# An experts' stage on TensorE: its order written down, and its weights read in longer rows

## The chip, the cores and the metric

The kernel runs on one core of a Trainium2 chip. The metric is device time of one execution in microseconds. The kernel before takes 2113.49 us, the median of three runs (2113.06 to 2113.59).

Engines are called by their short names in the profile: PE is TensorE (PEld its loading of the stationary operand), DVE is VectorE, ACT is ScalarE, POOL is GpSimd, SP is the engine that issues nearly all DMAs.

## The reference, cut to what matters

Two transformer-like blocks follow each other on 512 tokens of width 1024, all in float32. The first block (attention of two kinds, then a mixture of experts) holds the change. Its experts' part, per token block:

```python
    grp_probs = jax.nn.softmax(jnp.dot(x2, w_rg).astype(jnp.float32) + b_rg.astype(jnp.float32), axis=-1)
    grp = jnp.argmax(grp_probs, axis=-1)
...
    top_val, top_idx = lax.top_k(in_grp, TOP_K_IN_GROUP)
    gate = jax.nn.softmax(top_val, axis=-1) * p_grp[:, None]
...
    def run_block(args):
        tok, g, e = args
        xb = x2[tok]
        hb = jax.nn.silu(xb @ w_gate[e]) * (xb @ w_up[e])
        return (hb @ w_down[e]) * g[:, None].astype(x2.dtype)
...
    return jnp.zeros_like(x2).at[slot_tok].add(y_blocks.reshape(n_slots, -1))
```

`x2` is the normalised residual (`rmsnorm(h, g_ffn)`). Each token takes the best 2 of the 8 experts of its best group, of 4 groups; there are 32 experts, `run_block` is done on the tokens of one of them, `w_gate` and `w_up` are 1024 x 512 for each, `w_down` is 512 x 1024. The result is added to the residual `h`.

## The kernel before, in words

**Tiling.** The residual `h` is kept on chip, 4 chunks of 128 tokens by 1024 columns. Each expert has 64 places for tokens; a branch (L1246) with a general loop stands by for an expert that gets more, and is not taken with these inputs. The stage (`moe`, L1174) works on two experts at once, `p` from 0 to 15 (L1393): expert `2p` in columns 0 to 63 of the PE array, expert `2p+1` in columns 64 to 127, each product written with its place (`tile_position`). One product of a column half is two PE instructions in the trace, since the data is float32.

**One pass.**
- On even `p`: `onehots` (L1359) makes on DVE the 0/1 matrices that say which token sits in which place, for four experts, with the gates in `og2`; `gather` (L1375) multiplies the normalised tokens, kept as two parts `mnh` and `mnl`, by them (64 whole products, L1383 and L1384) and writes `xg`, the tokens of four experts with features on the partitions, scaled by the gain vector `gcol` (ACT, L1386). For `p` = 0 this was done ahead (`xg0`, L1212).
- PE transposes `og2` (L1409); DVE takes from it the gates `gs` and the 0/1 matrix `ohT` (L1411, L1413).
- Gate and up products (L1423), `j` = 0 and 1, 8 steps `k` over the features and two halves `i`. The queue of unfinished `units` is emptied between them, one after every second `k` (L1428).
- ACT makes silu of the gate product (L1435), DVE multiplies it by the up product (L1438), PE transposes the result in 4 blocks (L1441), DVE copies them to `aT` (L1443).
- Down products (L1451) in two column halves `n` of the output, 4 steps `f` and two halves `i`. ACT and DVE split the result into `yh` and `yl` (L1453, L1454).
- Each of the 8 `units` of a pass is an `add_back` (L1302): two whole products (L1306, L1307) that spread the experts' rows back to the tokens, and a DVE addition to `h` (L1308). Their PSUM banks have the tag `c`, two of them.

The last pass also prepares the final norm: rows of gains (`gain_rows`), and `last_rows` and `last_sums`, which take the place of `add_back`.

**What sets the order.** The program is written with a scheduler that reorders the instructions of each engine by its own simulated time, unless they are marked to be kept in program order. `in_order` (L191) marks all PE instructions inside it; in the stage before, only the end of the last pass (L1501) is inside it.

**Weights.** `pieces` (L1180) yields the weights of a pass as 12 tiles of 128 partitions by 2048 floats (1 MB each): gate and up in two halves `r` of 512 features for each expert, down in two column halves `n`. `load_w` (L103) reads each as 4 rows of 512 floats per partition, 2 KB at a time; feature `128 k + q` lies on partition `q`. `fetch` (L1192) issues them on the SP queue into a ring of 16 buffers (`ring_tile`, L92), 16 ahead of the stage and then 12 a pass; an issue waits until the last product that reads the buffer's old tile is done.

**Ahead of the stage.** At the start of the kernel `phase1` (L312) issues on the SP queue, in this order: `x` (4 DMAs), two weight tiles, the vectors `g_mix`, `sb_gain`, `hg_gain` and `g_ffn` as rows of 128 floats into `raw` (L363), the meta tokens `xm` (L399), `lg` (L401), and the next weight tiles. PE turns `raw` once (L394) so that the vectors lie along the partitions in `vec1`. `gcol` is a piece of it (L1077). `chunk` (L968) ends with the normalised copies `mnh` and `mnl` (L1004 to L1009).

Of the kernel before, what the change touches and what calls it, by code (L numbers as in the profile page):

```python
# [18 lines left out]
P = 128  # L19
# [292 lines left out]
def phase1(g, I, dbg):  # L312
# [49 lines left out]
    for o, (name, n) in ((0, ("g_mix", 8)), (8, ("sb_gain", 4)), (12, ("hg_gain", 4)), (16, ("g_ffn", 8))):  # L362
        nc.sync.dma_start(raw[o:o + n, :], rows128(I[name], n))  # L363
    rt0 = pn.tile([P, 1], F32, name="rt0")
# [603 lines left out]
    def chunk(c, ns, banks):  # L968
# [30 lines left out]
        if 1 in ns:  # L999
            V.scalar_tensor_tensor(g.L[:, c], pl, rs, g.br, op0=OP.mult, op1=OP.add)  # L1000
            if g.mnh is None:
                g.mnh = mixp.tile([P, NT, D], F32R, name="mnh", tag="mix")
            mnh = g.mnh
            nc.scalar.activation(mnh[:, c], h[:, c], AF.Copy, scale=rs)  # L1004
            for n in range(2):
                v = slice(512 * n, 512 * n + 512)
                t = latel.tile([P, 512], F32, name="mnt")
                nc.scalar.activation(t, h[:, c, v], AF.Copy, scale=rs)
                nc.gpsimd.tensor_tensor(mnl[:, c, v], t, mnh[:, c, v], op=OP.subtract)  # L1009
# [38 lines left out]
def route_consts(g, I):  # L1048
# [28 lines left out]
    g.gcol = g.vec1[:, g.o_gffn:g.o_gffn + KD]  # L1077

# [95 lines left out]
def moe(g, I, h, dbg):  # L1174
    nc, tc = g.nc, g.tc
    V = nc.vector
    st, gcol = g.mst, g.gcol
    g.ringc = st.enter_context(tc.tile_pool(name="ringc", bufs=NC, side="right"))

    def pieces():  # L1180
        for p in range(NE // 2):
            for src in ("w_expert_gate", "w_expert_up"):
                for r in range(2):
                    for e in (2 * p, 2 * p + 1):
                        yield (I[src], r * 4 * P, 4, FF, 0, FF, e * D * FF)
            for n in range(2):
                for e in (2 * p, 2 * p + 1):
                    yield (I["w_expert_down"], 0, 4, D, 512 * n, 512, e * D * FF)
# [57 lines left out]
    with tc.If(cnt > CAP):  # L1246
# [13 lines left out]
        with tc.For_i(0, NE, 1) as e:  # L1260
# [4 lines left out]
            wsrc = [I[n][0, bass.ds(e, 1)].rearrange("o (k p) n -> p (o k) n", p=P)  # L1265
                    for n in ("w_expert_gate", "w_expert_up", "w_expert_down")]
            for f in range(4):
# [4 lines left out]
                nc.sync.dma_start(w1, wsrc[0][:, :, fs])  # L1272
                nc.sync.dma_start(w2, wsrc[1][:, :, fs])
# [118 lines left out]
    units = []  # L1392
    for p in range(NE // 2):  # L1393
        if len(wq) < 12:
            fetch(12 - len(wq))
        ws, wq = wq[:12], wq[12:]
        if p % 2 == 0:
            og2 = onehots(p // 2)
            xg = gather() if p else xg0
            if p == NE // 2 - 2:  # L1400
                mn_st.close()

                hpp = tt_st.enter_context(tc.tile_pool(name="hpp", bufs=1, side="right"))
                hp = {}
                tt = g.mixp.tile([P, NT, D], F32, name="tt", tag="mix")
# [8 lines left out]
        last = p == NE // 2 - 1  # L1414
# [3 lines left out]
        gu, rows = [], []  # L1418
        for j in range(2):
            ps = pp.tile([P, FF], F32, name=f"pgu{j}", tag=f"gu{j}")  # L1420
            for k in range(KD):
# [6 lines left out]
                if units and (k % 2 or last):  # L1428
                    add_back(*units.pop(0))
# [5 lines left out]
        nc.scalar.activation(a, gu[0], AF.Silu)  # L1435
        if p == NE // 2 - 1:
            nc.scalar.activation(fs[:, 0, 0, 0:1], a[:, 0:1], AF.Sqrt, bias=g.eps, scale=0.0)
        V.tensor_mul(a, a, gu[1])  # L1438
# [4 lines left out]
        V.tensor_copy(aT, pt)  # L1443
        yh = wk.tile([P, D], F32R, name="yh")
        yl = wk.tile([P, D], F32R, name="yl")
        for n in range(2):
            ns = slice(512 * n, 512 * n + 512)
            ps = pp.tile([P, 512], F32, name="py", tag="y", bufs=2)
            for f in range(4):
                for i in range(2):  # L1450
                    nc.tensor.matmul(ps[64 * i:64 * i + 64], aT[:, f, 64 * i:64 * i + 64], ws[8 + 2 * n + i][:, f],  # L1451
# [693 lines left out]
```

## Time and profile before

| what | value |
|---|---|
| median of the runs | 2113.49 us |
| the profiled execution | 2112.79 us |
| its span, first to last instruction | 2111.1 us |
| mean granted clock of PE | 0.994 |
| first gate product of the stage starts | 390.73 us |
| last row of down products ends | 948.8 us |
| SP's issues of experts' weights | 265.4 to 894.3 us, 192 tiles of 1 MB |

The span is measured from the first to the last instruction; the profiled execution's own time is 1.7 us longer. In the rows shown below, a timeline row is the start in us, the duration, the engine, the line, the operation and the tiles, the count of like instructions in a row, and in brackets the idle time before it and what ended it. A row of windows gives for each engine the busy time and number of instructions, then the granted clock, the share of the DMA engines and GB/s. A group row gives count, then busy time and mean ns, then idle time before. PE is listed as busy while a product is in flight, so two products at once count once.

### The profile page before, as it was taken

To read this page: it belongs to the slowest core of one execution; us is meant where nothing else is said; L and a number is where in the kernel's file an instruction comes from. 1 tells how busy PE (TensorE), PEld (TensorE's weight loads), DVE (VectorE), ACT (ScalarE), POOL (GpSimd) and SP (SyncE) were. 2 spreads that over 40 slices of the span, in tenths; PEclk is the share of its full clock that TensorE was granted. 3 is DMA by queue.
4 is the path that set the end of the run, shared out by engine and by line. 5 is a ranking of instruction groups with operands and counts; after the bars stand their busy time and mean duration, and the time that the engine had idled before them with its cause. 6 is when DMAs were issued, how large, how long until landed. Compare 5 with 4: busy or idle time off the path is not lost.

```text
span 2111.1 us, 25109 instructions
## 1 busy us (share of the span) xinstructions
PE 2043.9 (97%) x9841; PEld 1393.8 (66%) x9841; DVE 976.0 (46%) x1516; ACT 684.1 (32%) x1041; POOL 750.7 (36%) x490
## 2 busy tenths in 40 slices
PE   8999989899999999999999999999999999999998
PEld 6877547444434433437877777777788888888886
DVE  7265575534343334235666776665444672000112
ACT  5443664111001101115343443334462353222322
POOL 4555453000000000014555465554444344444442
PEclk9999999899999999999999999999999999999999
DMA  4311216799999999934444344444553243333221
GB/s 137 120 41 41 90 60 212 254 386 386 386 376 350 351 363 345 355 93 146 126 122 121 103 130 119 117 136 129 194 202 130 95 120 90 100 100 100 100 81 40
DMA packets 259355, 366.73 MB, mean 174 GB/s; under 512 B 16968, under 2 KB 127856, under 8 KB 259232
## 3 DMA queue, kind: packets, MB, share of 16 engines
q1 hardware_dynamic: 258736, 363.43, 51.5%
q8 instruction: 79, 1.29, 0.3%
q10 hardware_dynamic: 496, 1.64, 0.2%
q14 instruction: 44, 0.36, 0.1%
HBM read 343.53 MB, written 12.65 MB: 169 GB/s over the span
## 4 chain that ended last, share of the span: by engine, by line
PE 64%; DVE 11%; ACT 2%; issue 2%; POOL 1%; DMA 0%; SPq 0%; DVEq 0%; ACTq 0%; POOLq 0%
PE pgu L1423 12%; PE psg L126 7%; PE psg L127 7%; PE psg L128 7%; PE py L1451 5%; DVE xacc L1771 2%; PE pc L1306 2%; PE pcv L1744 2%; PE pc L1307 1%; PE px L1383 1%; DVE G L1840 1%; PE px L1384 1%; PE acctr L127 1%; PE acctr L126 1%; DVE xacc L1768 1%
## 5 line engine op out<-in xcount | busy, mean ns | idle before, releaser
L126 PE MATMUL psg<-xh,hi 128*128 128x512 f32 x1040 | 411.8, 396 | 2.5 <-DVE z L1785 2.4
L128 PE MATMUL psg<-xh,lo 128*128 128x512 f32 x1040 | 409.7, 394 | 1.2 <-POOL lo L121 1.2
L127 PE MATMUL psg<-xl,hi 128*128 128x512 f32 x1040 | 406.7, 391 | 0.0
L1625 POOL TENSOR_TENSOR lo<-w,hi 128x1024 fp32r<-128x1024 f32 (+1 forms) x125 | 304.9, 2441 | 240.2 <-ACT hi L1623 236.3
L121 POOL TENSOR_TENSOR lo<-w,hi 128x1024 fp32r<-128x1024 f32 x86 | 213.2, 2483 | 222.7 <-ACT hi L119 221.7
L1423 PE MATMUL pgu<-w,xg 128*64 128x512 f32 x1024 | 262.7, 604 | 5.1 <-PEq L1246 5.1
L1623 ACT ACTIVATE hi<-w 128x1024 fp32r<-128x1024 f32 (+1 forms) x125 | 131.0, 1050 | 325.7 <-PE psg L127 225.9
L128 PEld LDWEIGHTS psg<-xh,lo 128*128 128x128 f32 x1040 | 195.4, 188 | 44.8 <-issue 2.8
L127 PEld LDWEIGHTS psg<-xl,hi 128*128 128x128 f32 x1040 | 195.5, 188 | 44.3 <-issue 4.7
L126 PEld LDWEIGHTS psg<-xh,hi 128*128 128x128 f32 x1040 | 195.5, 188 | 43.6 <-DVE z L1785 3.4
L1320 POOL TENSOR_TENSOR hh<-x,hh 128x512 fp32r<-128x512 f32 x4 | 5.0, 1275 | 532.4 <-ACT hh L1319 532.4
L1423 PEld LDWEIGHTS pgu<-w,xg 128*64 128x64 f32 x1024 | 74.3, 137 | 145.3 <-issue 135.9
L1308 DVE TENSOR_TENSOR x<-x,pc 128x512 f32<-128x512 f32 x120 | 79.3, 685 | 134.2 <-PE pc L1307 134.2
L119 ACT CAST hi<-w 128x1024 fp32r<-128x1024 f32 x89 | 92.9, 1044 | 148.3 <-issue 54.8
L1451 PE MATMUL py<-w,aT 128*64 128x512 f32 x512 | 134.9, 599 | 1.9 <-DVE aT L1443 1.9
L2067 DVE TENSOR_TENSOR act<-act,psg 128x512 f32<-128x512 f32 x22 | 15.1, 688 | 208.3 <-PE psg L128 203.0
L1771 DVE SCALAR_TENSOR_TENSOR xacc<-xp,tsc,xacc 128x512 f32<-128x512 f32 x96 | 90.7, 945 | 2.4
L1453 ACT ACTIVATE yh<-py,gsl 128x512 fp32r<-128x512 f32 x32 | 21.9, 688 | 208.4 <-PE py L1451 201.3
L1451 PEld LDWEIGHTS py<-w,aT 128*64 128x64 f32 x512 | 38.5, 136 | 72.8 <-issue 65.4
L1454 DVE SCALAR_TENSOR_TENSOR yl<-py,gsl,yh 128x512 fp32r<-128x512 f32 x32 | 23.9, 749 | 98.0 <-ACT yh L1453 98.0
L1768 DVE TENSOR_SCALAR xacc<-xp,tsc,tb 128x512 f32<-128x512 f32 x32 | 49.1, 1534 | 41.5 <-ACT xp L1766 37.0
L1843 POOL TENSOR_TENSOR G<-G,cb 128x512 f32<-128x512 f32 x32 | 50.5, 1595 | 39.9 <-ACT G L1842 25.4
(791 smaller groups left out, 3624.7 us busy)
## 6 DMA issues: line engine op xcount, KB each, us to landing
w<-in_w_expert_down_dram SPq DMA_DIRECT2D x64, 1024.0 KB, 10.5
w<-in_w_expert_gate_dram SPq DMA_DIRECT2D x64, 1024.0 KB, 8.6
w<-in_w_expert_up_dram SPq DMA_DIRECT2D x64, 1024.0 KB, 8.5
w<-in_w_in_dram SPq DMA_DIRECT2D x38, 1024.0 KB, 5.7
w<-in_w_gate_up_dram SPq DMA_DIRECT2D x44, 512.0 KB, 5.3
w<-in_w_in_dram SPq DMA_DIRECT2D x32, 512.0 KB, 4.2
w<-in_w_down_dram SPq DMA_DIRECT2D x11, 1024.0 KB, 4.8
vs<-vp SPq DMA_DIRECT2D x128, 67.5 KB, 2.0
```

The costliest lines, as they stand in the source:

```text
L119: (hi_on or nc.scalar.copy)(hv, w)
L121: (nc.vector if after else nc.gpsimd).tensor_tensor(lv, w, hv, op=OP.subtract)
L126: nc.tensor.matmul(ps, ah, bh, start=first, stop=False)
L127: nc.tensor.matmul(ps, ah, bl, start=False, stop=False)
L128: nc.tensor.matmul(ps, al, bh, start=False, stop=last)
L1308: V.tensor_add(h[:, c, ns], h[:, c, ns], ps)
L1423: nc.tensor.matmul(ps[64 * i:64 * i + 64], xg[k // 4][:, k % 4, q0 + 64 * i:q0 + 64 * i + 64], ws[4 * j + 2 * (k // 4) + i][:, k % 4], sta ...
L1451: nc.tensor.matmul(ps[64 * i:64 * i + 64], aT[:, f, 64 * i:64 * i + 64], ws[8 + 2 * n + i][:, f], start=(f == 0), stop=(f == 3), tile_posi ...
L1623: nc.scalar.activation(wh, wv, AF.Copy)
L1625: nc.gpsimd.tensor_tensor(wl, wv, wh, op=OP.subtract)
L1768: V.tensor_scalar(acc, xp[:, 0:T], tsc[:, ct:ct + 1], tb[:, o_scb + ct:o_scb + ct + 1], op0=OP.mult, op1=OP.add)
L1771: V.scalar_tensor_tensor(acc, xp[:, k:k + T], tsc[:, 32 * k + ct:32 * k + ct + 1], acc, op0=OP.mult, op1=OP.add)
```

## The change

It does four things.

1. All PE instructions of the stage stand inside `in_order`. The loop is rewritten so that its program order is the order wanted: 16 pairs of gate and up products; two `add_back`s of the pass before; the four transposes; on odd passes the `gather` for the next two passes; the other six `add_back`s; the transposes of the one-hots for the next pass (`put_back`); the down products. In the last pass the `add_back`s still stand between the gate products. `add_back` uses the banks `y` and `c` in turn, `aT` is copied by ACT instead of DVE, and the one-hots for the next passes are made on odd passes. Before the first pass stand `onehots(0)` and `put_back(0)`.
2. Each weight tile is read as 8 KB in a row per partition: for gate and up, feature `4 q + k` of a half lies on partition `q`; for down, a tile holds two steps `f` of both column halves.
3. To match this, the normalised copies, silu and the product with it are read or written with columns in steps of four.
4. The gain vector is needed in the new order too: two more DMAs read `g_ffn` into `raw`, 4 rows of 128 floats each, taken 4 floats apart; `gcolx` is that piece of `vec1`.

```diff
@@ phase1
+    for r in range(2):
+        nc.sync.dma_start(raw[24 + 4 * r:28 + 4 * r, :], dap(I["g_ffn"], 512 * r, [[1, 4], [4, P]]))
@@ chunk
-            nc.scalar.activation(mnh[:, c], h[:, c], AF.Copy, scale=rs)
+            nc.scalar.activation(mnh[:, c].rearrange("p (r k q) -> p r k q", r=2, k=4),
+                                 h[:, c].rearrange("p (r q k) -> p r k q", r=2, k=4), AF.Copy, scale=rs)
...
@@ moe
     def fetch(n):
-        for a in todo:
-            src, row0, kt, rowlen, col0, ncol, off = a
-            wq.append(load_w(g, src, row0, kt, rowlen, col0, ncol, off=off))
+        for src, off, row, kt in todo:
+            t = ring_tile(g)
+            nc.sync.dma_start(t, dap(src, off, [[row, P], [1, 2048]]))
+            wq.append(t.rearrange("p (k n) -> p k n", k=kt))
...
-    def add_back(ohT, yh, yl, n, c):
+    def add_back(ohT, yh, yl, n, c, tags=True):
-        ps = pp.tile([P, 512], F32, name="pc", tag="c", bufs=2)
+        i = g.n_back = g.n_back + 1
+        ps = pp.tile([P, 512], F32, name="pc", tag="yycc"[i % 4] if tags else "c", bufs=2)
...
+    order = in_order(g)
+    order.__enter__()
+    og2, xg = onehots(0), xg0
+    back = put_back(0, og2)
+    for p in range(np_):
...
+        if p % 2 and not last:
+            og2 = onehots(p // 2 + 1)
...
-                if units and (k % 2 or last):
-                    add_back(*units.pop(0))
+                if units and last:
+                    add_back(*units.pop(0), tags=False)
...
-        nc.scalar.activation(a, gu[0], AF.Silu)
+        av = a.rearrange("p (k q) -> p k q", k=4)
+        nc.scalar.activation(av, gu[0].rearrange("p (q k) -> p k q", k=4), AF.Silu)
...
-        V.tensor_mul(a, a, gu[1])
+        V.tensor_mul(av, av, gu[1].rearrange("p (q k) -> p k q", k=4))
+        for u in units[:2]:
+            add_back(*u)
         pt = pp.tile([P, 4, P], F32, name="pt", tag="g", bufs=2)
         for f in range(4):
             nc.tensor.transpose(pt[:, f], a[:, f * P:(f + 1) * P], g.ident)
-        V.tensor_copy(aT, pt)
+        nc.scalar.copy(aT, pt)
+        if p % 2 and not last:
+            xg = gather()
+        for u in units[2:]:
+            add_back(*u)
+        units = []
+        if not last:
+            back = put_back(p + 1, og2)
...
                 for i in range(2):
-                    nc.tensor.matmul(ps[64 * i:64 * i + 64], aT[:, f, 64 * i:64 * i + 64], ws[8 + 2 * n + i][:, f],
+                    nc.tensor.matmul(ps[64 * i:64 * i + 64], aT[:, f, 64 * i:64 * i + 64], ws[8 + 2 * (f // 2) + i][:, f % 2, ns],
                                      start=(f == 0), stop=(f == 3), tile_position=(0, 64 * i))
...
+    order.__exit__(None, None, None)
```

`put_back` holds what stood at L1406 to L1413: the transposes of the one-hots, `gs` and `ohT`. The general loop behind the branch of L1246 follows the new row order too, and is not taken.

More of the change, by code (lines that the diff above doesn't have):

```diff
@@ L1077, in route_consts @@
     g.gcol = g.vec1[:, g.o_gffn:g.o_gffn + KD]
+    g.gcolx = g.vec1[:, g.o_gffn + KD:g.o_gffn + 2 * KD]
 def route_tiles(g, I):
@@ L1176, in moe @@
     V = nc.vector
[L1177 removed]
+    st, gcol = g.mst, g.gcolx
     g.ringc = st.enter_context(tc.tile_pool(name="ringc", bufs=NC, side="right"))
@@ L1184, in pieces @@
                     for e in (2 * p, 2 * p + 1):
-                        yield (I[src], r * 4 * P, 4, FF, 0, FF, e * D * FF)
-            for n in range(2):
+                        yield I[src], e * D * FF + r * 512 * FF, 4 * FF, 4
+            for i in range(2):
                 for e in (2 * p, 2 * p + 1):
-                    yield (I["w_expert_down"], 0, 4, D, 512 * n, 512, e * D * FF)
+                    yield I["w_expert_down"], e * D * FF + 2 * i * D, 4 * D, 2
     todo = pieces()
@@ L1264, in moe @@
             nc.sync.dma_start(ge_, gsd[bass.ds(e, 1)].rearrange("o p c -> (o p) c"))
-            wsrc = [I[n][0, bass.ds(e, 1)].rearrange("o (k p) n -> p (o k) n", p=P)
-                    for n in ("w_expert_gate", "w_expert_up", "w_expert_down")]
+            wsrc = [I[n][0, bass.ds(e, 1)].rearrange("o (r p k) n -> p (o r) k n", p=P, k=4)
+                    for n in ("w_expert_gate", "w_expert_up")]
+            wsrc.append(I["w_expert_down"][0, bass.ds(e, 1)].rearrange("o (k p) n -> p (o k) n", p=P))
             for f in range(4):
@@ L1271, in moe @@
                 w3 = wk.tile([P, D], F32, name="ow3", tag="og_")
-                nc.sync.dma_start(w1, wsrc[0][:, :, fs])
-                nc.sync.dma_start(w2, wsrc[1][:, :, fs])
+                for w, src in ((w1, wsrc[0]), (w2, wsrc[1])):
+                    for r in range(2):
+                        nc.sync.dma_start(w[:, 4 * r:4 * r + 4], src[:, r, :, fs])
                 nc.sync.dma_start(w3, wsrc[2][:, f, :])
@@ L1391, in moe, with put_back @@
     p3.r1 = g.const.tile([P, NT], F32, name="r1")
[L1392 to L1405, printed above, removed]
+    def put_back(p, og2):
         q0 = P * (p % 2)
@@ L1413, in moe @@
         V.tensor_scalar(ohT, pt.rearrange("p c t -> p (c t)"), 0.0, None, op0=OP.not_equal)
-        last = p == NE // 2 - 1
+        return ohT, gs
+    np_ = NE // 2
+    units, rows = [], []
+    order = in_order(g)
[3 more added lines that the diff above has]
+    for p in range(np_):
+        if len(wq) < 12:
+            fetch(12 - len(wq))
+        ws, wq = wq[:12], wq[12:]
+        ohT, gs = back
+        last = p == np_ - 1
+        if p % 2 and not last:
+            og2 = onehots(p // 2 + 1)
+        q0 = P * (p % 2)
         if last:
             gfr = gain_rows("tg", 2, "og_")
-        gu, rows = [], []
+        gu = []
         for j in range(2):
@@ L1442, in moe @@
         aT = wk.tile([P, 4, P], F32, name="aT")
-        V.tensor_copy(aT, pt)
+        nc.scalar.copy(aT, pt)
[6 more added lines that the diff above has]
+            back = put_back(p + 1, og2)
+        if p == np_ - 3:
+            mn_st.close()
+            hpp = tt_st.enter_context(tc.tile_pool(name="hpp", bufs=1, side="right"))
+            hp = {}
+            tt = g.mixp.tile([P, NT, D], F32, name="tt", tag="mix")
         yh = wk.tile([P, D], F32R, name="yh")
```

6 lines of the change are left out of this document (4 added, 2 removed).

## The prediction

> **What bounds the kernel now.** I read the page first (how busy each engine is), then the busy time by window of the experts' stage, then what TensorE waits for, and last the single instructions of a pass.
>
> ```profile
> PE 2043.9 (97%) x9841; PEld 1393.8 (66%) x9841; DVE 976.0 (46%) x1516; ACT 684.1 (32%) x1041; POOL 750.7 (36%) x490
> ```
>
> ```profile
> 390.70:584.80 194.10, 193.90 (x898) 84.20 (x898) 78.42 (x152) 22.21 (x41) 0.00 (x0) 0.99 1.01 371
> ...
> 729.80:872.60 142.80, 138.43 (x611) 57.24 (x610) 50.67 (x93) 14.39 (x29) 0.00 (x0) 1.00 0.99 354
> ...
> sum 558.10, PE 545.58 PEld 227.09 DVE 207.09 ACT 61.86 POOL 9.27; mean PE 136.39 PEld 56.77 DVE 51.77 ACT 15.46 POOL 2.32
> ```
>
> ```profile
> PEld pgu L1423 <- DMA w<-in_w_expert_gate_dram: 1.1, 3, 0.4
> ```
>
> The first row says TensorE (PE) is busy 97% of the span. The windows cut the experts' stage, from its first gate product to its last down product: 558.1 us, and PE is busy in nearly all of it, the DMA share is 1 throughout, and 354 to 371 GB/s arrive. Two resources look full, so the wait decides: in the whole stage PE waited 1.1 us for weights. The stage is PE's, and the DMA queue runs close behind it. But busy PE is not PE at its peak, so next its instructions.
>
> ```profile
> 915.66 0.40 PE L1306 MATMUL pc<-yh,ohT 128*128 128x512 f32 x1
> 915.90 0.40 PE L1307 MATMUL pc<-yl,ohT 128*128 128x512 f32 x1
> 916.23 1.07 PE L1423 MATMUL pgu<-w,xg 128*64 128x512 f32 x2
> 917.23 0.50 PE L1306 MATMUL pc<-yh,ohT 128*128 128x512 f32 x1
> 917.56 0.40 PE L1307 MATMUL pc<-yl,ohT 128*128 128x512 f32 x1
> ```
>
> ```profile
> 549.53 1.08 PE L1423 MATMUL pgu<-w,xg 128*64 128x512 f32 x4
> 550.54 0.50 PE L1307 MATMUL pc<-yl,ohT 128*128 128x512 f32 x1
> ```
>
> ```profile
> 482.85 6.87 PE py L1451 x32
> ```
>
> A product over 64 columns is two instructions, and the two column halves (one expert each) run at the same time: 32 instructions, 16 products, take 6.87 us in the chain, so two instructions fill one slot of 6.87/16 = 0.429 us. Four instructions, a product for each half, occupy PE from 549.53 to 550.54, 1.01 us. Two instructions, a product of one half alone, take 916.23 to 917.23, 1.00 us: the same. So a product whose partner stands elsewhere takes two slots alone; next to its partner the two share them, and each lone product brought back saves one slot, 0.429 us. A change between half products and whole ones costs too: 1.01 - 2 x 0.429 = 0.15 on leaving, 917.56 - 917.23 - (915.90 - 915.66) = 0.09 for the first whole one, and 916.23 - 915.90 - 0.24 = 0.09 on the way back, 0.33 us a round trip.
>
> **The change, part by part.** First the work, which stays.
>
> ```profile
> L1423 PE MATMUL pgu<-w,xg 128*64 128x512 f32 x1024 | 262.7, 604 | 5.1 <-PEq L1246 5.1
> L1451 PE MATMUL py<-w,aT 128*64 128x512 f32 x512 | 134.9, 599 | 1.9 <-DVE aT L1443 1.9
> L1383 PE MATMUL px<-oh,mnh 128*128 128x256 f32 x224 | 56.0, 287 | 0.0
> ...
> L1306 PE MATMUL pc<-yh,ohT 128*128 128x512 f32 x120 | 54.3, 462 | 0.0
> ...
> L1441 PE MATMUL pt<-ident,act 128*128 128x128 f32 x64 | 10.3, 283 | 8.8 <-DVE act L1438 8.8
> ```
>
> ```profile
> 511.64 0.28 PE L1383 MATMUL px<-oh,mnh 128*128 128x256 f32 x1
> ...
> 514.94 0.28 PE L1383 MATMUL px<-oh,mnh 128*128 128x256 f32 x1
> ```
>
> ```profile
> 401.04 1.07 PE L1423 MATMUL pgu<-w,xg 128*64 128x512 f32 x2
> ...
> 945.15 3.65 PE L1451 MATMUL py<-w,aT 128*64 128x512 f32 x14
> ```
>
> Half products: (1024 + 512)/2 = 768 slots, 329.5 us. Adding back (L1306 and its twin L1307): 240 x 0.24 = 57.6. Gather (L1383 and its twin L1384): 448 at (514.94 - 511.64)/28 = 0.118, 52.9. Transposes and gain rows, 160 by the loops at 0.12 (four end 0.66 after the first starts, the last taking some 0.3, in a row below), 19.2. The last pass's sums, 16 x 0.24 and 8 x 0.43, 7.3. Together 466.5, so 91.6 of the 558.1 us is not work. Going through PE's timeline I count 86 products without partner (the second of these fences holds the first and the last stretch that ends in one; an x14 is three pairs and one alone) and 121 changes: 86 x 0.429 = 36.9 and 121 x 0.33 = 39.9. The wait between gate product and transposes adds about 12 times 0.89, 10.7:
>
> ```profile
> 893.95 0.69 DVE L1438 TENSOR_TENSOR act<-act,pgu 128x512 f32<-128x512 f32 x1 [2.87 <-PE pgu L1423]
> 894.69 0.66 PE L1441 MATMUL pt<-ident,act 128*128 128x128 f32 x4 [0.89 <-DVE act L1438]
> ```
>
> ```profile
> 390.73 10.12 PE L1423 MATMUL pgu<-w,xg 128*64 128x512 f32 x34 [5.11 <-PEq L1246]
> ...
> 394.80 0.42 DVE L1372 TENSOR_TENSOR og__4153<-og__4153,ot__4166 128x256 f32<-128x256 f32 x1
> ```
>
> Written order. The new loop runs per pass: gate and up products in pairs, two add-backs, four transposes, the gather (odd passes), six add-backs, the one-hots' transposes, then the down products, which run straight into the next pass's gate products. That is one round trip a pass, and some 13 in the last pass, which keeps its interleaving: 28 for 121, saving 93 x 0.33 = 30.7. All products are paired: 36.9. Two add-backs (4 x 0.24 = 0.96, and 0.15 on leaving) stand where PE waited 0.89, so ten of the twelve waits go: 8.9. The first pass has no add-backs and the last none left. Saved: 76.5 us.
>
> What strict order adds. Before the first gate product now stand the one-hots' transposes; DVE finishes those one-hots at 395.2, PE began at 390.73, so with four transposes 5.1 us more. In each of 14 passes VectorE's 0.69 and its latency may end 0.2 after the two add-backs: 2.8. The last pass's closing sums stand behind all its down products, so their chain on other engines is covered less: 3 (nothing to 4 slots of a half, 3.4). Added 10.9. The copy moved to ScalarE has at least six add-backs ahead of its reader (2.9 us for about 0.7). VectorE's eight adds are 0.69 each against 0.48 of PE, and four banks instead of two hold the lead; the down products behind give it 6.9 us to catch up. The strided reads I cost at nothing beside the same contiguous form: they hide behind add-backs, at 0.7 us a pass if they doubled. The normalised copies ahead of the stage may add 0 to 5; I take 1. Stage: 558.1 - 76.5 + 10.9 = 492.5.
>
> Weights read 8 KB in a row.
>
> ```profile
> DMA packets 38861, 77.29 MB, mean 386 GB/s; under 512 B 1177, under 2 KB 1177, under 8 KB 38852
> ```
>
> ```profile
> DMA packets 747, 2.91 MB, mean 415 GB/s; under 512 B 37, under 2 KB 37, under 8 KB 747
> ```
>
> These are the queues from 400 to 600 us (packets of 2 KB, sixteen engines full) and from 213 to 220 (packets of 4 KB): longer packets, higher rate. PE's 492.5 us needs 176 tiles of 1.049 MB behind the 16 that are there, plus about 18 us (first release, one-hots, latency, the last half product): at 386 GB/s 176 x 2.72 + 18 = 496, DMA would bind; at 415 176 x 2.53 + 18 = 463, covered by 29. I take 415 as the nearest row; the bound of 386 costs 4 to 10 with the ring's sixteen slots. All four down tiles are now held to the end of the down products, which is inside that cover.
>
> Here the Trainium skill speaks against the change: DMA: Bandwidth & Descriptors, section Bandwidth, gives about 358 GB/s as the limit of the memory side of one core. By it a tile would take 2.93 us and the stage 533; the rows above, 386 and 415, do not agree with it, and the measurement decides.
>
> The gain vector read in strides. To match the new row order the kernel loads `g_ffn` twice more, each load 4 rows of 128 single 4-byte elements, in the first microseconds.
>
> ```profile
> DMA packets 1714, 0.01 MB, mean 0 GB/s; under 512 B 1714, under 2 KB 1714, under 8 KB 1714
> ```
>
> ```profile
> dsk<-in_d_skip_dram SPq DMA_DIRECT2D x2, 4.0 KB, 22.8
> ```
>
> ```profile
> DMA packets 246, 0.58 MB, mean 292 GB/s; under 512 B 56, under 2 KB 80, under 8 KB 246
> ```
>
> ```profile
> 5.87 0.27 SPq L363 DMA_DIRECT2D vec_raw<-in_g_ffn_dram  x1
> ...
> 11.50 3.60 SPq L105 DMA_DIRECT2D w<-in_w_in_dram  x2
> ```
>
> ```profile
> 36.81 1.05 ACT L119 CAST hi<-w 128x1024 fp32r<-128x1024 f32 x1 [7.30 <-PE pst L128]
> ```
>
> ```profile
> 61.10 1.05 ACT L119 CAST hi<-w 128x1024 fp32r<-128x1024 f32 x1 [5.19 <-DMA w<-in_w_in_dram]
> ```
>
> The trace has such a load: `dsk`, 2048 single elements, 22.8 us to landing. From 36 to 52 us only they move, 1714 in 16 us: on sixteen engines 0.149 us an element. And loads of few rows use few engines: from 12.9 to 14.9 us 56 packets are under 512 B, which is a count of landings (16 for a full tile, 8 + 4 + 4 + 8 for the four vector loads by their rows, 16 for the next). So each new load gives four engines 128 elements: 19 us if the two loads use different engines, 38 if the same. I take 38, as two loads alike have nothing to choose differently. DMA: Bandwidth & Descriptors, section Why a DMA increments its semaphore by 16 and not by 1, has the same rule and names the lowest-numbered engines, by which it is 38; the landings agree with the first half, no run here shows the second.
>
> They stand on the SP queue between `g_ffn` at 5.87 and the third and fourth weight tiles at 11.50; whatever is behind them waits on those four engines. The third tile is first cast at 36.81, so some 20 us of the delay are covered there; the fifth was already waited for (ACT idle 5.19 us at 61.10), so hardly anything covers it there, and PE is full up to the stage. Bounds 0 to 38; I take 34.
>
> Sum: 2112.79 (the profiled execution; 2111.1 of span and 1.7 around it, 0.7 under the median 2113.49) - 76.5 + 10.9 + 1 + 34 = 2082.
>
> **The rivals.** First, the start costs nothing: single elements may be slow in `dsk` because all its rows read the same 128 bytes of memory, and then the new loads pass in a few us under the cover of 36.81. Against it: fixed steps of 0.15 us on every engine look like the price of a write, not of one crowded address. Time 2048. Second, longer rows bring no higher rate: the DMA binds at 386 GB/s, the stage ends at 496 to 503, time 2086 to 2092. Third, on the other side: long rows fall to the 354 GB/s of the later stage, since each engine then reads one far place at a time; a tile takes 2.96 us, the stage 176 x 2.96 + 18 = 539, time 2112.79 - 19 + 35 = 2129. It decides below 366 GB/s, where 176 tiles and 18 us eat all but the 35 us lost elsewhere. The 358 of the Trainium skill would lie on that side. For it: the 354 row; against: there the ring's free slots set the pace, and 415 at 4 KB. Fourth, strict order meets a wait that I do not see in each pass (a bank held by VectorE's adds, a copy queued behind the gather's), 2 us in 16 passes: 2114. Against: every engine but PE is busy under half of the stage.
>
> **How the numbers follow.** The forecast 0.50, the first rival 0.30, the second 0.05, the third 0.07, the fourth 0.08. About 0.2% (4 us) is what a measurement here can tell from no change. Faster by more: 0.50 + 0.30 + 0.05 and a third of the fourth, 0.88; within: 0.04; slower: 0.08. The range goes from the first rival with 12 us of a better stage (no 0.2 waits, 0.35 a round trip, no loss at the end), 2036, to the forecast with the DMA's bound, the full 38 and half of the fourth rival, 2108.
>
> **What would show it.** Right: between the first gate product and the last down product about 490 us; gate products in unbroken stretches of 64 and the down products joined on, one change a pass; DMA packets of 8 KB at 400 GB/s or more; ScalarE's cast now at 36.81 waiting for a DMA until about 60, and the stage starting about 34 us later than 390.7. Wrong: a stage start near 390 (first rival); waits of PE for `w` in the stage (second, third); PE idle before the transposes or down products in each pass (fourth).

## The result and the profile after

The kernel after takes 2046.97 us, the median of four runs (2045.94 to 2048.62); the kernel before, on the same chip, 2113.27 us. The ratio is 0.9688, with a 95% interval of 0.9671 to 0.9704: 66 us faster, where 31 were forecast. The profiled execution took 2046.73 us, its span is 2045.0. Of the times on record the first rival's, 2048 us for a start that costs nothing, is the nearest; how much of that is chance is said further down.

The page's first part, then the windows of the stage of the kernel after, again from its first gate product to its last down product (inside `in_order` every product now carries the line of the wrapper, L197, so products are told apart by tile):

```profile
PE 1979.2 (97%) x9841; PEld 1396.8 (68%) x9841; DVE 961.5 (47%) x1500; ACT 702.4 (34%) x1057; POOL 749.1 (37%) x490
```

```profile
593.80:783.80 190.00, 190.00 (x982) 92.90 (x982) 83.76 (x162) 27.41 (x51) 0.00 (x0) 1.00 1.01 419
...
sum 473.50, PE 472.16 PEld 222.72 DVE 181.85 ACT 69.19 POOL 5.10; mean PE 157.39 PEld 74.24 DVE 60.62 ACT 23.06 POOL 1.70
```

The stage fell from 558.1 to 473.5 us, by 84.6. PE's share of the span is the same 97% as before: the number that looked full says nothing of how well it was filled. The groups and the timeline of one pass of the kernel after:

```profile
L197 PE MATMUL pgu<-w,xg 128*64 128x512 f32 x1024 | 227.6, 599 | 0.0
...
L197 PE MATMUL py<-w,aT 128*64 128x512 f32 x512 | 113.6, 596 | 0.2 <-ACT aT L1467 0.2
```

```profile
429.34 13.90 PE L197 MATMUL pgu<-w,xg 128*64 128x512 f32 x64
443.17 0.50 PE L197 MATMUL pc<-yh,ohT 128*128 128x512 f32 x1
443.51 0.39 PE L197 MATMUL pc<-yl,ohT 128*128 128x512 f32 x1
...
444.20 0.60 PE L197 MATMUL pt<-ident,act 128*128 128x128 f32 x4
```

The same instructions, one by one 600 ns long as before, keep PE busy for 227.6 + 113.6 us instead of 262.7 + 134.9, since two are in flight all the time: of the 1536, none is without partner now (86 products, 172 instructions, were), and PE changes between half and whole products 30 times instead of 121. The gate and up products stand in one stretch of 64, then the two add-backs, then the transposes.

The waits of PE from the stage's start to its end and a little beyond, first after, then before:

```profile
PE pst L197 <- DVE dg L1526: 6.7, 1, 6.7
PE pt L197 <- DVE og__4163 L1386: 6.3, 4, 5.1
PE pt L197 <- DVE act L1459: 1.1, 2, 0.9
```

```profile
PE pt L1441 <- DVE act L1438: 8.8, 10, 0.9
PE pgu L1423 <- PEq L1246: 5.1, 1, 5.1
PE py L1451 <- DVE aT L1443: 1.9, 6, 0.3
...
PE pst L197 <- DVE dg L1488: 1.5, 1, 1.5
```

Eight of the ten waits for `act` are gone. At the ends stand a new one, for the one-hots ahead of the first gate product, and a longer one, for the diagonals `dg` behind the last down product. The DMA queue of 440 to 640 us in the kernel after moves 8 KB packets at 417 GB/s, and no product of PE waits for `w` (the loading of the stationary operand, PEld, does 11 times in the stage, 3.2 us together, where it did for 1.1 before):

```profile
DMA packets 11449, 83.45 MB, mean 417 GB/s; under 512 B 1271, under 2 KB 1271, under 8 KB 1271
```

At the start, SP's timeline and the two casts that stood at 36.81 and 61.10 before:

```profile
7.70 6.07 SPq L366 DMA_DIRECT2D vec_raw<-in_g_ffn_dram  x2
13.81 2.78 SPq L402 DMA_DIRECT2D xm<-in_meta_tokens_dram  x1
16.64 0.42 SPq L404 DMA_DIRECT2D lg<-in_lb_logits_dram  x1
```

```profile
40.16 1.05 ACT L119 CAST hi<-w 128x1024 fp32r<-128x1024 f32 x1 [7.28 <-PE pst L128]
```

```profile
64.47 1.05 ACT L119 CAST hi<-w 128x1024 fp32r<-128x1024 f32 x1 [5.76 <-DMA w<-in_w_in_dram]
```

Both casts are 3.4 us late, not 34, and the first still waits for PE, not for a DMA. The strided loads hold SP for 6.07 us, and `xm` and `lg` go out later by 6 to 8. But what reaches the chain comes another way, through PE's one transposition of `raw`, the tile that the loads write. First before, then after:

```profile
15.20 0.30 PE L394 MATMUL psv<-ident,vec_raw 128*128 128x128 f32 x1 [0.34 <-DMA vec_raw<-in_g_ffn_dram]
```

```profile
18.27 0.45 PE L397 MATMUL psv<-ident,vec_raw 128*128 128x128 f32 x1 [3.27 <-DMA vec_raw<-in_g_ffn_dram]
```

PE stands idle for 3.27 us there, and the products behind it are as late. The transposition of `xm` does not make PE wait in either trace. The prediction looked at what stands behind the loads on the queue, not at what reads their tile.

Where the 66 us went, in the order of the kernel (the pieces are the shifts of PE's products, counted through both traces):

| piece | forecast | measured |
|---|---|---|
| the two strided gain loads at the start | +34 | +3.4 |
| normalised copies ahead of the stage | +1 | +6.8 |
| one-hots ahead of the first gate product | +5.1 | +2.9 |
| the stage, first gate to last down product | -73.7 | -84.6 |
| behind the last down product | +3 | +5.4 |
| sum | -30.6 | -66.1 |

The stage's forecast is the 76.5 saved less the 2.8 of new waits. Some work only changed its place: ten whole products of the last pass, 2.8 us by the prediction's prices, stood in the stage before and stand behind it now. The first gate product starts at 403.8 instead of 390.7, which is the first three pieces; the end is 1167.7 us behind the last down product instead of 1162.3.

### The profile page after: what moved, and what is told of

Its sections match the earlier page's. It is cut to its first block, busy times and chain, and to the rows that moved or that the text cites. A ratio compares the mean times of both kernels' runs of the same rounds, so it can differ in the third digit from the quotient of the medians.

```text
span 2045.0 us, 25143 instructions
## 1 busy us (share of the span) xinstructions
PE 1979.2 (97%) x9841; PEld 1396.8 (68%) x9841; DVE 961.5 (47%) x1500; ACT 702.4 (34%) x1057; POOL 749.1 (37%) x490
## 4 chain that ended last, share of the span: by engine, by line
PE 64%; DVE 9%; ACT 3%; issue 2%; POOL 2%; SPq 0%; DMA 0%; DVEq 0%; ACTq 0%; POOLq 0%
PE pgu L197 11%; PE psg L126 7%; PE psg L127 7%; PE psg L128 7%; PE py L197 6%; PE pc L197 3%; PE px L197 3%; DVE xacc L1809 2%; PE pcv L1782 2%; DVE G L1878 1%; PE acctr L126 1%; PE accy L126 1%; PE acctr L127 1%; PE acctr L128 1%; PE accy L127 1%
## 5 line engine op out<-in xcount | busy, mean ns | idle before, releaser
L197 PE MATMUL pgu<-w,xg 128*64 128x512 f32 x1024 | 227.6, 599 | 0.0
L197 PEld LDWEIGHTS pgu<-w,xg 128*64 128x64 f32 x1024 | 73.1, 138 | 144.3 <-issue 141.8
L197 PE MATMUL py<-w,aT 128*64 128x512 f32 x512 | 113.6, 596 | 0.2 <-ACT aT L1467 0.2
L1459 DVE TENSOR_TENSOR act<-act,pgu 128x512 f32<-128x512 f32 x16 | 11.0, 688 | 187.4 <-PE pgu L197 187.4
L197 PEld LDWEIGHTS py<-w,aT 128*64 128x64 f32 x512 | 35.4, 137 | 67.6 <-issue 65.4
```

What stands on the lines that cost most here:

```text
L197: return lambda *a, **k: tc.keep_in_program_order(f(*a, **k))
```

## The experiments

All twelve were timed beside the kernel before, each beside it on one chip; ratios are to that kernel (0.9688 for the kernel after). 1% is 21 us.

**The start alone.** The kernel before, with only the two loads added:

```diff
+    for r in range(2):
+        nc.sync.dma_start(raw[24 + 4 * r:28 + 4 * r, :], dap(I["g_ffn"], 512 * r, [[1, 4], [4, P]]))
```

> The kernel before with one thing added: the two strided loads of g_ffn, whose result nobody reads. The prediction's step (0.149 us for each single element on each of four engines) gives +34 us, 2147 us, and ScalarE's cast at 36.81 us waiting for a DMA until about 60. The theory from the two traces: an element costs its engine about 8 ns and only SP's issue of the two loads (6.07 us in the trace after) stands in the way of what is behind it on the queue, of which 3.4 us arrive at TensorE: 2113.3 + 3.4 = 2116.7 us, the cast at about 40.2. A third view, that these loads cost nothing by themselves and the 3.4 us come from elsewhere in the change, gives 2113.

2116.46 us, ratio 1.0022 (1.0013 to 1.0031), so 2.7 to 6.5 us more. Its cast, and SP's issue of the two loads:

```profile
40.39 1.05 ACT L119 CAST hi<-w 128x1024 fp32r<-128x1024 f32 x1 [7.30 <-PE pst L128]
```

```profile
7.23 6.53 SPq L365 DMA_DIRECT2D vec_raw<-in_g_ffn_dram  x2
```

The 34 us are refuted by themselves, without the rest of the change. The loads do cost something, but the path was another than the expectation's: PE's transposition reads the new rows of `raw` too, though nobody uses what comes of them, and waits 3.26 us for the loads, as in the kernel after. SP's issue takes as long as there (6.53 us for 6.07).

**Why `dsk` was slow.** The prediction's price came from the loads of `dsk`. Here, in the kernel before, they read 2048 different places of another tensor (other numbers, so the skip gains of the second block are not the reference's):

```diff
-        nc.sync.dma_start(q.dsk[64 * a:64 * a + 64, :], dap(I["d_skip_2"], a, [[0, 64], [2, 16]]))
+        nc.sync.dma_start(q.dsk[64 * a:64 * a + 64, :], dap(I["w_in"], a, [[64, 64], [2, 16]]))
```

> The kernel before with dsk read from 2048 distinct addresses (rows of w_in, 256 bytes apart, instead of the same 128 bytes for each of 64 rows), so the skip gains of the second block are other numbers here. Theory: the 0.149 us per element from which the prediction worked out 34 us is the price of many reads of one place in memory: the stretch in which only single elements move (36 to 52 us) shrinks to a few us, the weight tile behind it lands earlier, ScalarE's wait of 5.19 us at 61.1 goes, total 2108 to 2111 us. Rival (the prediction's step): it is the price of any single element on its engine, nothing changes: 16 us of single elements, 2113 us.

2111.21 us, ratio 0.9995 (0.9986 to 1.0005). The DMA of 37 to 52 us of the kernel before, then of 35 to 37 us of this one, and this one's cast:

```profile
DMA packets 1607, 0.01 MB, mean 0 GB/s; under 512 B 1607, under 2 KB 1607, under 8 KB 1607
```

```profile
DMA packets 2133, 0.01 MB, mean 4 GB/s; under 512 B 2133, under 2 KB 2133, under 8 KB 2133
```

```profile
60.12 1.05 ACT L119 CAST hi<-w 128x1024 fp32r<-128x1024 f32 x1 [5.12 <-issue]
```

2133 single elements passed in 2 us, where 1607 had taken 15: about 0.015 us an element on each of sixteen engines instead of 0.149. The price belonged to 64 rows that read the same 128 bytes, as the first rival said. And the time did not change: the cast once credited with a wait of 5.19 us for a DMA starts 1.0 us earlier and still has 5.12 us of idle time ahead of it, for which the profile names no releaser. My expectation of 2 to 5 us was wrong in that.

**The rows alone**, in the order of before (the diff of pieces 2, 3 and 4 of the change, with the old loop):

> The kernel before, order of TensorE as it was, with all that belongs to reading the weights 8 KB in a row: the new row order of the weights, the strided gain loads, the permuted normalised copies and gate products. Theory: the experts' stage is TensorE's, so it stays at 558 us although the weights arrive at 415 GB/s or more; the start costs 3.4 and the doubled copies (ScalarE 1.15 to 2.12 and 0.71 to 1.21 us) cost some 7 before the stage: 2113.3 + 10 = 2123 to 2124 us. Rival: the DMA held the stage back too (share 1.01 of the time), and the rows alone bring a good part of the 66 us: 2080 to 2110, the stage under 550.

2135.57 us, ratio 1.0110 (1.0094 to 1.0125): slower, and by more than the 10 us expected. The stage of this kernel in one window:

```profile
396.90:965.60 568.70, 555.12 (x2397) 231.76 (x2398) 203.13 (x373) 59.61 (x111) 5.04 (x4) 1.00 0.85 331
```

The DMA share fell to 0.85 and the stage did not get shorter, 568.6 us: DMA was not what held it. The first gate product is 6.2 us late, the stage 10.5 longer and the part behind it longer by 6.2. The scheduler, which is free here, laid PE's products in another order: passes of 41.2 and 33.5 us in place of 37.2 and 34.2, and ten more products behind the last down product. The trace has 114 products without partner, 28 more than the kernel before, and 123 changes for 121; 28 x 0.429 = 12.0 us, so the lost partners alone explain the longer stage. Why the scheduler ordered so was not followed up.

**The order alone**: the kernel after with the old 2 KB reads, and no permuted copies or gains:

```diff
...
-            t = ring_tile(g)
-            nc.sync.dma_start(t, dap(src, off, [[row, P], [1, 2048]]))
+            src, row0, kt, rowlen, col0, ncol, off = a
+            wq.append(load_w(g, src, row0, kt, rowlen, col0, ncol, off=off))
...
```

> The kernel after with the weights read as before (2 KB in a row, no strided gain, no permuted copies), TensorE's written order kept. Theory: the order needs 473 us, but 176 tiles at 386 GB/s and 18 us around them need 497, so TensorE now waits for weight tiles in the stage: 473 to 497 us, with the start and the copies given back (3.4 + 7): 2047 - 10 + 0 to 24 = 2037 to 2061 us, and I expect waits of TensorE for w of 10 us or more. Rival: the rows bring nothing that the order needs, the queue delivers as fast as it is asked: no waits for w, 2036 us, faster than the kernel after.

2063.83 us, ratio 0.9776 (0.9761 to 0.9791). Its waits of PE, its stage and its queue from 440 to 640 us:

```profile
PE pgu L197 <- DMA w<-in_w_expert_up_dram: 12.8, 8, 1.6
...
PE pgu L197 <- DMA w<-in_w_expert_gate_dram: 4.3, 3, 1.6
```

```profile
396.10:894.60 498.50, 480.05 (x2394) 225.70 (x2393) 182.21 (x344) 69.11 (x126) 5.08 (x4) 1.00 1.03 377
```

```profile
DMA packets 38835, 77.27 MB, mean 386 GB/s; under 512 B 1178, under 2 KB 1178, under 8 KB 38824
```

Now PE waits 17.1 us for weights, and the stage is 498.5 us, between the 496 and 503 that the prediction's second rival gave for 386 GB/s. The written order made the DMA the bound, and the longer rows are what that order needs: 25 us in the stage, of which 7.7 are lost ahead of it, to the copies and loads that they ask for. Neither half of the change is worth 66 us alone: the rows by themselves lose 23, the order by itself gains 47.

**The pairs.** In the first 512 columns of the down products, one expert's four products and then the other's:

```diff
-            for f in range(4):
-                for i in range(2):
+            for f, i in ([(f, i) for i in range(2) for f in range(4)] if n == 0 else
+                         [(f, i) for f in range(4) for i in range(2)]):
```

> The kernel after with one order changed: in the first 512 columns of the down products all four products of one expert, then all four of the other, in place of pairs. Theory: TensorE overlaps two column halves only when they stand next to each other, so 16 passes x 4 pairs need two slots more each, less about one slot at each place where the halves meet: 16 x (16 - 8 - 1) slots... by slots 16 x 8 = 128 at most, 16 x 7 = 112 at least, at 0.429 us: 48 to 55 us more, 2095 to 2102 us. Rival: TensorE's queue finds the other half by itself a few instructions later, or the two slots of a lone product were a wait of another kind: 2047 us.

2075.11 us, ratio 0.9824 (0.9806 to 0.9842): 29 us more, between the two theories. The stage took 501.4 us, 27.9 more. PE's timeline where the down products of one pass meet the gate products of the next:

```profile
463.61 0.59 PE L197 MATMUL py<-w,aT 128*64 128x512 f32 x1
463.67 0.59 PE L197 MATMUL pgu<-w,xg 128*64 128x512 f32 x1
464.04 0.59 PE L197 MATMUL py<-w,aT 128*64 128x512 f32 x1
464.10 0.59 PE L197 MATMUL pgu<-w,xg 128*64 128x512 f32 x1
```

The second expert's last down products run at the same time as the first expert's gate products of the next pass. A half that lags finds partners further on: 8 instructions a pass run alone instead of 16. The count in the trace is 832 slots instead of 768, and 64 x 0.429 = 27.5 us: the price of a slot holds, but a product without neighbour is not always a product without partner.

**The changes.** Six of the eight add-backs of each middle pass go back between the gate pairs; no pair is broken:

```diff
                 if units and last:
                     add_back(*units.pop(0), tags=False)
+                elif units and k % 2 and len(units) > 2:
+                    add_back(*units.pop(0))
```

> The kernel after with six of the eight add-backs of each middle pass put back between gate pairs, one behind every second pair; all pairs stay pairs, nothing is added. Theory: each change between half and whole products and back costs 0.33 us: 14 passes x 6 x 0.33 = 28 us more, and up to 5 more where the copy of the activations loses its cover in passes without a gather: 2075 to 2080 us. Rival: the changes cost nothing, the whole gain of the order came from the pairs and the waits: 2047 us.

2079.89 us, ratio 0.9840 (0.9825 to 0.9855). Its stage, and its longest wait of PE there:

```profile
403.60:910.20 506.60, 503.21 (x2394) 209.76 (x2393) 190.67 (x344) 69.18 (x126) 5.09 (x4) 1.00 0.91 372
```

```profile
PE py L197 <- ACT aT L1469: 2.3, 8, 0.3
```

The stage is 33.1 us longer with 84 changes more, 114 for 30. 2.1 us are the copy `aT` that lost its cover (2.3 for 0.2), 0.9 are two products of the last pass that stand alone in this trace; the rest is 30.1/84 = 0.36 us a change. The prediction had 0.33. Counted in the trace a round trip is 0.35: 0.10 more than a slot to leave a half, 0.10 more for the first whole product, 0.09 on the way back, and 0.05 because the first slot of a half behind a change takes 0.48 us instead of 0.429. The last is inside the prediction's 0.15 (1.01 us are 0.48 + 0.43 + 0.10).

**The copies.** In the kernel before and in the kernel after, the normalised copies of one chunk:

```profile
357.62 1.15 ACT L1004 ACTIVATE mnh<-x,rsn 128x1024 fp32r<-128x1024 f32 x1
358.67 0.71 ACT L1008 ACTIVATE mnt<-x,rsn 128x512 f32<-128x512 f32 x1
```

```profile
362.55 2.12 ACT L1008 ACTIVATE mnh<-x,rsn 128x1024 fp32r<-128x1024 f32 x1
364.58 1.20 ACT L1013 ACTIVATE mnt<-x,rsn 128x512 f32<-128x512 f32 x1
```

Reading `h` with a step of 16 bytes takes 1.8 and 1.7 times as long, twelve on ACT, and the copies of the first three chunks start 7.8 to 7.9 us apart instead of 6.4 to 6.5. Four ways were tried. First, contiguous copies, with PE loading every fourth column as its stationary operand:

```diff
...
-                    nc.tensor.matmul(px[:, k, :], mnh[:, c, ks], rt.oh[c], start=(c == 0), stop=False)
+                    nc.tensor.matmul(px[:, k, :], every4(mnh, c, 2 * kk + k), rt.oh[c], start=(c == 0), stop=False)
...
```

> The kernel after with the two normalised copies written as before (contiguous reads); the permutation is made where TensorE loads the copies as stationary operand, every fourth column, 64 loads before the stage and 448 in the gathers. Theory: the copies alone put 7 us between the start and the stage (ScalarE's reads with a step of 16 bytes take 2.12 instead of 1.15 us and 1.21 instead of 0.71): the stage begins at about 397 instead of 403.8, total 2047 - 7 = 2040 us, if a strided load of the stationary operand costs nothing more than 0.19 us. Rival: the strided stationary load doubles as ScalarE's read did, 0.19 to 0.38 us against a product of 0.118 every time: the 448 of the gathers grow by up to 0.07 to 0.19 each, 30 to 85 us: 2070 or more.

2097.70 us, ratio 0.9932 (0.9918 to 0.9946): the rival, 52 us more. A gather product then starts every 0.235 us instead of 0.118:

```profile
445.75 0.40 PE L201 MATMUL px<-oh,mnh 128*128 128x256 f32 x1
445.99 0.40 PE L201 MATMUL px<-oh,mnl 128*128 128x256 f32 x1
```

Second, contiguous reads and strided writes:

```diff
-            nc.scalar.activation(mnh[:, c].rearrange("p (r k q) -> p r k q", r=2, k=4),
-                                 h[:, c].rearrange("p (r q k) -> p r k q", r=2, k=4), AF.Copy, scale=rs)
+            nc.scalar.activation(mnh[:, c].rearrange("p (r k q) -> p r q k", r=2, k=4),
+                                 h[:, c].rearrange("p (r q k) -> p r q k", r=2, k=4), AF.Copy, scale=rs)
...
```

> The kernel after with the normalised copies permuted by a strided write instead of a strided read: ScalarE reads in a row and writes with a step of 512 bytes from element to element. Theory: it is the read with a step of 16 bytes that halves the rate (2.12 against 1.15 us, 0.24 doubled to 0.235 per gather product in the run before this one): 1.15 and 0.71 us again, the stage about 4 us earlier, 2043 us. Rival: ScalarE pays for the stride on either side: 2.12 and 1.21, 2047 us.

(The "0.24" in it is a slip for 0.118.) 2046.71 us, ratio 0.9694 (0.9681 to 0.9708), the same as the kernel after: a copy took 2.11 us. So ScalarE took as long with the step of 512 bytes in its writes as with 16 bytes in its reads. Third, gate and up weights 4 KB in a row, two rows of the matrix per partition, which asks for a step of 8 bytes only; with it the gains are loaded by one DMA behind the router's weights, as pieces of 8 bytes:

```diff
-                        yield I[src], e * D * FF + r * 512 * FF, 4 * FF, 4
+                        yield I[src], e * D * FF + r * 512 * FF, [[2 * FF, P], [256 * FF, 2], [1, 1024]], 4
...
+    nc.sync.dma_start(g.gcolx.rearrange("p (s k) -> p s k", k=2), dap(I["g_ffn"], 0, [[2, P], [256, 4], [1, 2]]))
```

> The kernel after with gate and up weights read 4 KB in a row (two rows of the matrix per partition instead of four; the down weights stay at 8 KB), so the normalised copies and the gains are permuted with a step of 8 bytes instead of 16, and the gains loaded by one load behind the router's, straight into place. Theory: ScalarE's read halves because each 16 bytes of memory give it one number; with a step of 8 bytes they give two and the copies take 1.15 and 0.71 us again; that brings about 4 us, the load behind the router's about 3, and 4 KB packets still feed the stage (415 GB/s, 463 us of 473): 2046.5 - 7 = 2039 to 2040 us. Rival: ScalarE pays for any step that is not 4 bytes: 2.1 and 1.2 us, 2043 us, with the stage beginning near 400. Third: 4 KB packets do not reach 400 GB/s in the stage, and TensorE waits for w there: 2045 us or more.

2037.61 us, ratio 0.9652 (0.9638 to 0.9665), 7.6 us less than the kernel after by the ratios. Its copies, and its queue from 440 to 640 us:

```profile
361.75 1.24 ACT L1005 ACTIVATE mnh<-x,rsn 128x1024 fp32r<-128x1024 f32 x1
362.90 0.74 ACT L1010 ACTIVATE mnt<-x,rsn 128x512 f32<-128x512 f32 x1
```

```profile
DMA packets 17761, 82.40 MB, mean 412 GB/s; under 512 B 1254, under 2 KB 1254, under 8 KB 14167
```

1.24 and 0.74 us, nearly the contiguous figures, and 412 GB/s are enough: its stage is 473.6 us long. With the loads out of `raw`, PE's transposition of it starts at 14.96 us, 3.3 earlier than in the kernel after. Fourth, the same rows with contiguous copies and PE loading every second column:

> The run beside this one (4 KB in a row) with the normalised copies contiguous, and TensorE loading every second column of them as stationary operand, in the gathers too. Theory: what doubled the gather with every fourth column (0.118 to 0.235 us a product) was that each 16 bytes gave one number; every second column gives two and costs nothing: gather products at 0.118, 2039 us, the same as the run beside it. Rival: a stationary operand that does not lie in a row is loaded at half the rate whatever its step: 0.235, 52 us more, 2091 us.

2039.06 us, ratio 0.9657 (0.9642 to 0.9671), the gather at 0.12 us a product:

```profile
437.08 0.29 PE L201 MATMUL px<-oh,mnh 128*128 128x256 f32 x1
437.20 0.29 PE L201 MATMUL px<-oh,mnl 128*128 128x256 f32 x1
```

So it is not the stride as such: with one number out of every 16 bytes ScalarE takes 1.8 times as long and PE's gather twice as long, with two both lose next to nothing.

**The two ends of the order.** In the first pass the one-hots' transposes stand behind the gate and up products; in the last, the closing sums of the first 512 columns stand in the middle of the last down products:

```diff
-    back = put_back(0, og2)
...
+        ohT, gs = back if p else put_back(0, og2)
         for u in units[:2]:
             add_back(*u)
...
+                if last and n and f == 1:
+                    for c in range(NT):
+                        last_sums(c, 0, rows[c], ohT, yh, yl)
+                        squares(c, 0, rows[c])
```

> The kernel after with the written order loosened at both ends: in the first pass the one-hots' transposes stand behind the gate and up products instead of ahead of them, and in the last pass the closing sums of the first 512 columns stand in the middle of the down products of the second. Theory: the order put 5.4 us ahead of the stage (403.8 against 398.4; the run with the order alone began at 396.1 where the kernel before began at 390.7) and some 5 us behind it (the chain on VectorE and GpSimd that follows the last down product starts late): 2046.5 - 5 - 3 to 5 = 2036 to 2039 us. Rival: the waits only move: VectorE's one-hots then hold up the transposes of the first pass, and VectorE's squares, not the sums, set the end: 2044 to 2047 us.

2038.78 us, ratio 0.9654 (0.9641 to 0.9668), 7.2 us less than the kernel after. PE at its first pass:

```profile
397.03 15.52 PE L197 MATMUL pgu<-w,xg 128*64 128x512 f32 x64 [2.97 <-ACTq L1255]
412.48 0.66 PE L197 MATMUL pt<-ident,og__4163 128*128 128x128 f32 x4
413.41 0.66 PE L197 MATMUL pt<-ident,act 128*128 128x128 f32 x4 [0.28 <-DVE act L1457]
414.70 0.63 PE L197 MATMUL pt<-ident,og__4163 128*128 128x128 f32 x4 [0.63 <-DVE ohT L1415]
```

The stage starts at 397.0, is 475.4 us long (two short waits and one change more), and the end stands 1163.4 us behind the last down product, 4.3 less than 1167.7. Both costs were of the strict order.

**Together**: the third way of the copies and the loosened ends.

> The kernel after with both sets of edits that shortened it: gate and up weights 4 KB in a row with the gains loaded late (8.8 us less against the run beside it, by the ratios 0.9688 and 0.9652 about 7.6), and the order loosened at both ends (ratio 0.9654, about 7.2). Theory: they lie at different places of the chain (start, copies, first pass, last pass), so the gains add up: 2112 x 0.9688 - 7.6 - 7.2 = 2031 us. Rival: they overlap, since the earlier normalised copies and the later one-hots both move the same start of the stage, so that only one of the two counts there: 2034 to 2036 us.

2030.77 us, ratio 0.9620 (0.9607 to 0.9633): the gains add up, and this kernel is 80 us faster than the kernel before and 14 faster than the kernel after. From the last product of the first gather to the first gate product its trace has 4.0 us, where the 4 KB rows alone had 8.1: the looser first pass still counts at the start, against the rival.

## Why the prediction was wrong, step by step

**The step that failed** is "on sixteen engines 0.149 us an element", carried from `dsk` to the new loads, and with it "I take 34". The arithmetic was sound, the row was not alike: `dsk` reads the same 128 bytes for 64 rows, the new loads read each of 1024 elements once. The loads alone cost 2.7 to 6.5 us, the trace after shows 3.4, which reach PE through the transposition of `raw`, a wait that the prediction did not look for, and `dsk` from different places passes in 2 us. The rival that said so had 0.30, and the argument against it, that fixed steps on every engine look like the price of a write, was wrong: both kinds write single elements.

The second half of the same step, that the fifth tile's cast has no cover because it "was already waited for", is not borne out either: in the run with `dsk` from different places nothing blocks the queue, and the cast keeps its idle time and the kernel its length. A releaser in a row says which event came last, not that an earlier event would have helped.

That the first rival's 2048 us lies 1 us from the measured 2047 is partly luck. It was right that single elements are not slow as such. But the start was not free, and it moved to 403.8, not to near 390 as that rival's sign had it; start, copies and end cost 11.6 us more than in its sum, and stage and one-hots 13.1 less.

**Lone products, 36.9 us.** Right: 86 before, none after, and 64 slots more, 27.5 us by the price, made the stage 27.9 longer when pairs were parted.

**Changes, 0.33 us.** Nearly right: 0.36 by the run with the changes put back. With that and 91 changes fewer (30 remain, 28 were forecast) they bring 32.8 instead of 30.7.

**Waits, 8.9 saved and 2.8 added.** The prediction's twelve waits of 0.89 are ten in the rows, 8.8 us together. The waits for `act` and `aT` fell from 8.8 + 1.9 to 1.1 + 0.2, 9.4 saved; the added 0.2 a pass did not come. With these the stage's gain is 36.9 + 32.8 + 9.4 = 79.1 of 84.6. Of the other 5.5, 3.3 are 14 whole products that now stand outside the stage (four transposes ahead of it, ten products behind it), at the prediction's prices, so they are moved and not saved; two waits of 0.8 in the last pass are gone, and one of 0.4 is new. About 1 us is not traced.

**One-hots, 5.1.** Right as a mechanism: with the order alone the first gate product came at 396.1, 5.4 us later than before. In the kernel after it was 2.9; why it was less there was not traced.

**Normalised copies, 1.** Mis-sized, 6.8: they lie on the chain that ends ahead of the stage. "Hide behind add-backs" was true of silu and the product in the stage, which read PSUM: silu took 597 ns against 598 before. It was not asked of the copies that read SBUF. The Trainium skill, SBUF - State Buffer, section Specifications (TRN2), gives the rule: lines of 16 bytes, and full rate only with at least two accesses to a line. The trace agrees, 2.12 us with one access and 1.24 with two, against 1.15 contiguous; it was overlooked.

**The end, 3.** 5.4: PE waited 6.7 us for `dg`, where it had waited 1.5, and did the ten moved products there; a wait of 1.6 for `yl` went.

**Rows, 415 GB/s.** 417, and PE did not wait for `w`. The statement that DMA "runs close behind" was right: without the longer rows it would have taken back 25 us. The 358 GB/s of the Trainium skill's DMA: Bandwidth & Descriptors, section Bandwidth, did not bind here, at 8 KB (417) as at mostly 4 KB (412). The prediction read that figure too narrowly: the same section gives it for both cores of the memory's domain streaming, and one core ran here.

The three terms that were too pessimistic (start by 30.6, stage by 10.9, one-hots by 2.2) outweigh the two that were too kind (copies by 5.8, end by 2.4): 43.7 - 8.2 = 35.5, which is 66.1 - 30.6. One sum of the prediction is off: the three gains named for the lower end of its range make 7.7 us at its own prices (2.8, 93 x 0.02 = 1.9, and 3), not 12, so that end would be 2040 and not 2036.

## What to carry to other kernels

Before a price is taken from a row of the trace, ask what else that row has that the new work has not; here a source of 128 bytes read by 64 rows, which made an element ten times dearer. Ask also what reads the tile that the new load writes. Where an engine is busy 97% of the time, look at how many of its instructions are in flight together: a written order that keeps column halves adjacent and changes between half and whole products once a pass shortened a stage of 558 us by 60 with the same instructions, and by 85 once longer rows fed it. The permutation that the longer rows ask for cost nothing where the operand lies in PSUM, next to nothing at two numbers per 16 bytes of SBUF, and nearly half the rate at one; and an order that is right in the middle of a loop should be loosened in its first and last pass.

## What the runs showed of the hardware that was not expected

- PE lets the column halves run apart by some products: the down products of one expert ran beside the gate products of the other, of the next pass.
- A stationary operand of every fourth column doubles the time between products (0.118 to 0.235 us); every second column costs nothing that matters (0.12).
- SP's issue of the two strided loads ended at 13.8 us in two kernels, though it began at 7.70 in one and at 7.23 in the other, so it waited for something. In the kernel after the DMA engines moved 383 GB/s from 10 to 13 us and 51 from 13 to 15, so it may have been the first tiles, still on the queue; that was not tested.
- Just ahead of the stage, PE's granted clock falls to 0.50, for longer in the kernel after. One row of windows of the kernel before, then two of the kernel after:

```profile
372.00:378.00 6.00, 6.00 (x30) 5.83 (x29) 4.23 (x26) 2.05 (x4) 2.55 (x2) 0.50 0.25 96
```

```profile
378.00:384.00 6.00, 5.56 (x26) 5.28 (x26) 3.82 (x20) 4.34 (x7) 1.28 (x1) 0.50 0.09 19
384.00:390.00 6.00, 4.64 (x23) 4.43 (x23) 5.56 (x33) 1.26 (x2) 1.29 (x1) 0.50 0.99 416
```

Part of the 6.8 us of the copies may be this: the products of the first gather start every 0.21 us there instead of 0.118. What holds the clock down was not tried.
